# State-space pipeline beside the projections, key selection regrouped and its passes pinned in a queue

## The chip, the core and the metric

The kernel runs on one core of a Trainium2 chip. The core has five engines, each with its own queue, worked off in order: TensorE (PE: matmuls and transposes; PEld in the profile is its weight load), VectorE (DVE), ScalarE (ACT), GpSimd (POOL), and SyncE (SP), which here only starts transfers. On-chip memory is SBUF, and PSUM for TensorE's results. The metric is the time of one execution in microseconds (us), as the median of several.

## The reference

One decoder block on 2048 tokens of 1024 channels, in float32: RMSNorm with adaptive shift and scale, one wide input projection, two branches, a gated merge, an output projection, and a SwiGLU feed-forward part.

```python
u = rms_norm(h, norm1_g[layer]) * (1.0 + scale1) + shift1
xs, q, ckv, qi, ki, wi, ga, gb = split_cols(u @ w_in[layer], IN_SIZES)
y_ssm = s5_branch(xs, ...)          # state-space branch
y_att = dsa_branch(q, ckv, qi, ki, wi, ...) @ w_attn_proj[layer]
merged = jax.nn.sigmoid(ga) * y_ssm + jax.nn.sigmoid(gb) * y_att
h = h + gate1 * (merged @ w_out[layer])
u2 = rms_norm(h, norm2_g[layer]) * (1.0 + scale2) + shift2
ffn = (jax.nn.silu(u2 @ w_ffn_gate[layer]) * (u2 @ w_ffn_up[layer])) @ w_ffn_down[layer]
```

The state-space branch is a diagonal linear recurrence over time in 32 groups of 16 channels (64 states each), then GELU, then a gated linear unit (`y @ w_glu`, "GLU" below). The attention branch selects keys first: per query, four small index heads give a score for every earlier key, and the 256 highest are kept:

```python
rel = jax.nn.relu(jnp.einsum('bqhd,bkd->bqhk', qi, k_idx))
iscore = jnp.einsum('bqhk,bqh->bqk', rel, wi)
_, sel = lax.top_k(iscore, topk)            # topk = 256
```

Attention with eight heads then runs over the selected keys alone.

## The kernel before, in words

Matmuls run in a fast float32 type; each operand is split in a high and a low part, so one product is three matmuls (`mm3`, high x high, high x low, low x high), all issued at line 102. The stages, in order of time:

1. **Input projections** (`main_A`). `w_in` is taken in column blocks of 128, the tokens in four quarters of 512. One output tile `pps` of 128x512 takes 24 matmuls (8 blocks of the contraction x 3) into one of three PSUM banks, and one eviction on ScalarE: `kraw`, `qio`, `xsT`, `craw` for keys, index queries, state-space input and latent, `qo` (L648) for queries, `go` (L654, a sigmoid) for the two gates `ga`, `gb`. There are 112 tiles. Weights come as `wraw` on SP's queue, are rounded to `wh` on ScalarE (L433), and `wl` is the rest, on GpSimd (L113). The tokens' operands are `U` and `Uh`.
2. **Key selection** (`select_group`, L730 on), for blocks of 128 queries, 2 to 15 (a block b sees (b+1) x 128 keys). Scores: `sps` on TensorE, relu `rl` on ScalarE (L713), weighted sum `SC` on VectorE (L718). Then a search for the threshold: in each pass ScalarE counts, row by row, the scores above a bound (`ja`, L766, a Sign with an accumulated sum, one instruction per block), and VectorE moves the bounds (`tsel`, L768 to L782, some twelve short instructions). Then the nearest scores (`near`, L800), and the mask (`gt`). Several blocks form a group that shares the short instructions; 11 passes per group, 14 for the smallest blocks. Two lists of groups run beside each other (`GROUPS`).
3. **State-space operators** (`ssm_build`): GpSimd multiplies (`sE`, `sT`, `sW`, `sO`), ScalarE and VectorE split them (`opt`), SP stores them to `scratch_opd` and `scratch_etd`.
4. **State-space pipeline** (`main_ssm`): 16 steps of two groups each ("pairs"), staged over eleven further steps. For a pair: loads of `sxc`, `oph`, `sEt` on SP, transposes `sxp`, split `XHL` (ScalarE, VectorE), matmuls `sup` (12), rotation `sZ` (VectorE, GpSimd), a scan along time on VectorE (`ZS`), `sP` (GpSimd), split `PHL`, matmuls `syp` (18), GELU `sY` (ScalarE, L1237), transposes `sbp` and `syt`, copies `YC` and `sy`.
5. **GLU** (`main_glu`, tiles `ggp`, `gvp`), then **attention**, **merge**, **feed-forward**.

What runs beside what is fixed while the program is written out. `beside(main, ...)` takes steps of a main generator and, for each, gives every background generator credit of its step's nominal time x a rate; a background runs while it has credit. `BR` is the rate of the operators, `SR` that of the two lists of groups, and the number that a step yields is what it is charged. A scheduler then puts each engine's instructions in order by a model of its own; it may move an instruction ahead of others that were written earlier. `keep_in_program_order` forbids that for one instruction: it stays behind the one that was written before it on its engine.

Before, projections run with the operators, both lists of groups, and `lead()`, which starts the pipeline's first ten yields when 14 or fewer steps of the projections are left. Then the pipeline runs on its own, then the GLU with what is left of selection.

Buffers come from rings of equal slots: `big` (tag p8, 9 slots of 8 KB per partition), `half` (h4, 27 of 4 KB), `qtr` (q2, 12 of 2 KB).

Of the kernel before, what the change touches and what calls it, by code (L numbers as in the profile page):

```python
# [36 lines left out]
BR = 0.6  # L37
SR = (0.55, 0.55)
# [6 lines left out]
LEAD = (14, 10, 6)  # L45
# [13 lines left out]
GROUPS = ((((7, 6), 11), ((15,), 11), ((13,), 11)), (((5, 4, 3, 2), 14), ((14, 12, 10), 11), ((11, 9, 8), 11)))  # L59


class Kernel:
# [667 lines left out]
    def select_group(self, bs, passes, then):  # L730
# [33 lines left out]
        for p in range(passes):  # L764
            for i in range(nb):
                A.activation(junk[:, :W_[i]], S_[i], AF.Sign, bias=T[:, 0, i:i + 1], accum_out=C[:, i:i + 1])  # L766
            yield sum(W_) * CTA + 0.1 * nb + 0.8
# [17 lines left out]
            yield 0.5  # L785
# [8 lines left out]
        for i in range(nb):  # L794
            W = W_[i]
            n = -(-W // 512)
            for c in range(n):
                s = S_[i][:, c * 512:min((c + 1) * 512, W)]
                y = self.qtr([128, 512], "near")[:, :s.shape[1]]
                A.activation(y, s, AF.Sign, bias=far[:, i:i + 1], scale=-1.0)  # L800
                V.scalar_tensor_tensor(y, y, FAR, s, op0=OP.mult, op1=OP.min)
                V.max(m8[:, nb + c if n > 1 else i], y)
            if n > 1:
                V.max(m8[:, i], m8[:, nb:nb + n])
            yield W * CFIN[0]
# [334 lines left out]
    def main_ssm(self):  # L1140
# [4 lines left out]
        def load(bt, kinds):  # L1145
            for kind in kinds:
                op[bt, kind] = t = self.half([128, 2, 4, 128], "oph", F32R)
                S.dma_start(t.bitcast(F32), self.opd[bt, :, kind].rearrange("p w (g x) -> p w g x", x=128))
# [8 lines left out]
        def split_x(p):  # L1157
            if p % 2 == 0:
                R = op[p // 2, 1].bitcast(F32)
                RS = self.half([128, 2, 4, 128], "RS", F32R)  # L1160
                G.tensor_scalar(RS[:, :, :, :64], R[:, :, :, 64:], 1.0, 1.0, op0=OP.mult, op1=OP.mult)
                G.tensor_scalar(RS[:, :, :, 64:], R[:, :, :, :64], -1.0, 1.0, op0=OP.mult, op1=OP.mult)
                op[p // 2, 4] = RS

# [1109 lines left out]
    def run(self, stop=99):  # L2274
        tc = self.tc
        self.stores, self.now, self.qpre, self.left, self.xsT = [], 0.0, {}, 99, {}
        with ExitStack() as st:
# [38 lines left out]
            def select(groups):  # L2316

                for g, (bs, passes) in enumerate(groups):
                    while self.seg < 1 or max(bs) >= 8 and (self.ready < 2 or self.E16 is not None):
# [30 lines left out]
            def lead():  # L2350

                while self.left > LEAD[0] or build[0] is not None:
                    yield None
                for _ in range(LEAD[1]):
                    yield next(ssm) * LEAD[2]

# [55 lines left out]
```

## Time and profile before

| | us |
|---|---|
| median of three runs | 3326.09 (3324.31 to 3326.35) |
| profiled execution | 3328.0 |
| its span (first to last instruction) | 3326.2 |
| TensorE busy | 3109.1 (93%) |
| VectorE busy | 2263.7 (68%) |
| ScalarE busy | 1558.8 (47%) |
| GpSimd busy | 1548.1 (47%) |
| projections, first matmul to end of last | 49.5 to 938.1 |
| pipeline, until the GLU's first matmul | 938.1 to 1062.9 |

TensorE's busy time counts overlapping matmuls as one stretch; a matmul's own duration (some 0.39 us for 512 columns) is longer than the distance to the next one. The granted clock (PEclk) is the share of its full rate that TensorE was given. A wait is put down to the instruction that ended it. In the views, "L102 PE" with a tile's name tells the stage, since every matmul has that line.

### The profile page before, as it was taken

Reading aid. Unit: us, or ns where it says so; the run is one execution under the profiler, and the core shown is the slowest. Engines: PE = TensorE matmul, PEld = TensorE weight load, DVE = VectorE, ACT = ScalarE, POOL = GpSimd, SP = SyncE. Lnnn points to the kernel's source line nnn. Section 1 sums busy time; section 2 is a strip of 40 time slices with the busy share of each in tenths; the row PEclk is TensorE's granted clock in tenths of the full one; section 3 lists DMA queues with packets and bytes.
Section 4 is the critical chain, followed back from the end, with each engine's and each line's share of the span. In section 5 each row is a group of like instructions: output and inputs, shape, how many; then the busy total and the mean of one; then the engine's idle time right before and its main releaser. Section 6 shows DMA issues by size and latency. Waiting matters only on the chain.

```text
span 3326.2 us, 44918 instructions
## 1 busy us (share of the span) xinstructions
PE 3109.1 (93%) x15346; PEld 2572.7 (77%) x15346; DVE 2263.7 (68%) x4617; ACT 1558.8 (47%) x2758; POOL 1548.1 (47%) x1200
## 2 busy tenths in 40 slices
PE   5988778999988999999989999999999999999998
PEld 2776656777877888888978887888878888888786
DVE  6778567866366848888974548666676666755576
ACT  3335656695644327888952234323333223332233
POOL 2465534623156656666651235555564545200533
PEclk8999889999998999999999999999999999999999
DMA  7533323564366771000154665333443333665464
GB/s 242 165 102 118 108 91 137 202 203 141 104 237 242 260 236 60 20 20 20 36 169 155 193 219 173 99 101 106 139 135 115 108 95 99 228 221 162 144 224 143
DMA packets 386680, 479.97 MB, mean 144 GB/s; under 512 B 38208, under 2 KB 264720, under 8 KB 384784
## 3 DMA queue, kind: packets, MB, share of 16 engines
q1 hardware_dynamic: 373200, 452.95, 42.1%
q10 hardware_dynamic: 13248, 24.12, 2.0%
q8 instruction: 121, 1.98, 0.2%
q14 instruction: 111, 0.91, 0.1%
HBM read 311.77 MB, written 165.22 MB: 143 GB/s over the span
## 4 chain that ended last, share of the span: by engine, by line
PE 65%; DVE 9%; DMA 5%; issue 4%; ACT 4%; POOL 3%; SPq 0%; ACTq 0%; DVEq 0%; POOLq 0%
PE fps L102 25%; PE dps L102 7%; PE wops L102 5%; PE pps L102 5%; PE aps L102 4%; PE pvo L102 4%; PE ptp L110 3%; PE apj L102 3%; PE ggp L102 3%; PE gvp L102 3%; DMA bw<-in_w_ffn_down_dram 2%; ACT ja L766 2%; DVE SC L718 1%; PE kps L102 1%; PE sps L102 1%
## 5 line engine op out<-in xcount | busy, mean ns | idle before, releaser
L102 PE MATMUL fps<-X,wp 128*128 128x512 f32 x3696 | 865.6, 396 | 11.1 <-POOL wp L113 4.1
L102 PEld LDWEIGHTS fps<-X,wp 128*128 128x128 f32 x3696 | 697.8, 189 | 175.7 <-POOL wp L113 5.0
L102 PE MATMUL pps<-Uh,wh 128*128 128x512 f32 x1120 | 361.8, 401 | 22.1 <-ACT qo L648 15.4
L102 PE MATMUL dps<-db,dh 128*128 128x512 f32 x1056 | 324.8, 390 | 6.2 <-ACT db L2053 5.0
L113 POOL TENSOR_TENSOR wl<-wraw,wh 128x1024 fp32r<-128x1024 f32 x72 | 180.2, 2505 | 301.4 <-ACT wh L433 251.6
L102 PEld LDWEIGHTS pps<-Uh,wh 128*128 128x128 f32 x1120 | 214.2, 193 | 69.1 <-ACT qo L648 15.9
L102 PE MATMUL pps<-U,wh 128*128 128x512 f32 x672 | 228.2, 419 | 39.4 <-ACT go L654 22.0
L766 ACT ACTIVATE ja<-SC,tsel 128x1152 int8<-128x1152 f32 (+11 forms) x166 | 210.2, 1268 | 85.4 <-DVE tsel L782 73.5
L102 PEld LDWEIGHTS dps<-db,dh 128*128 128x128 f32 x1056 | 197.7, 188 | 49.9 <-ACT db L2053 7.3
L113 POOL TENSOR_TENSOR wp<-wraw,wp 128x512 fp32r<-128x512 f32 x88 | 131.7, 1506 | 198.9 <-ACT wp L1911 198.9
L102 PE MATMUL pps<-Uh,wl 128*128 128x512 f32 x560 | 223.7, 400 | 0.0
L1518 POOL TENSOR_SCALAR P<-P,sum 128x1024 f32<-128x1024 f32 (+2 forms) x192 | 170.5, 900 | 83.8 <-DVE sum L1515 72.1
L102 PE MATMUL dps<-db,dl 128*128 128x512 f32 x528 | 204.3, 389 | 0.0
L113 DVE TENSOR_TENSOR pl<-ptp,ph 128x512 fp32r<-128x512 f32 (+1 forms) x288 | 183.9, 655 | 27.5 <-ACT ph L1572 25.2
L102 PEld LDWEIGHTS pps<-U,wh 128*128 128x128 f32 x672 | 133.1, 201 | 74.0 <-ACT go L654 22.8
L102 PE MATMUL wops<-wo,M 128*128 128x512 f32 x768 | 184.9, 397 | 0.0
L1959 POOL TENSOR_TENSOR c<-c,c 128x512 f32<-128x512 f32 x66 | 88.7, 1344 | 195.2 <-issue 133.5
L110 PE MATMUL ptp<-shift,P 128*128 128x128 f32 x1088 | 169.6, 278 | 10.2 <-POOL P L1518 6.7
L1572 ACT CAST ph<-ptp 128x512 fp32r<-128x512 f32 (+1 forms) x288 | 156.1, 563 | 49.0 <-PE ptp L110 45.0
L102 PE MATMUL aps<-K,Qh 128*128 128x512 f32 (+3 forms) x640 | 173.5, 378 | 2.6 <-DVE mx L1505 2.6
L102 PEld LDWEIGHTS wops<-wo,M 128*128 128x128 f32 x768 | 142.4, 188 | 32.0
L102 PE MATMUL pvo<-pl,Vt 128*128 128x256 f32 x576 | 165.5, 317 | 0.0
(455 smaller groups left out, 7128.1 us busy)
## 6 DMA issues: line engine op xcount, KB each, us to landing
draw<-scratch_hp SPq DMA_DIRECT2D x66, 512.0 KB, 4.6
bw<-in_w_ffn_down_dram SPq DMA_DIRECT2D x121, 256.0 KB, 3.9
wraw<-in_w_in_dram SPq DMA_DIRECT2D x56, 512.0 KB, 5.3
scratch_hp<-c SPq DMA_DIRECT2D x110, 256.0 KB, 2.0
wraw<-in_w_ffn_gate_dram SPq DMA_DIRECT2D x44, 512.0 KB, 6.4
wraw<-in_w_ffn_up_dram SPq DMA_DIRECT2D x44, 512.0 KB, 6.9
scratch_opd<-opt SPq DMA_DIRECT2D x32, 512.0 KB, 3.0
oph<-scratch_opd SPq DMA_DIRECT2D x32, 512.0 KB, 6.4
```

Source lines behind the costliest of these rows:

```text
L102: self.T.matmul(ps, lhsT, rhs, start=start, stop=stop)
L110: self.T.transpose(out, in_, self.ident)
L113: (eng or self.V).tensor_tensor(out, src, hi.bitcast(F32), op=OP.subtract)
L718: V.scalar_tensor_tensor(sc, r, self.WI[:, b, h:h + 1], sc if h else more, op0=OP.mult, op1=OP.add)
L766: A.activation(junk[:, :W_[i]], S_[i], AF.Sign, bias=T[:, 0, i:i + 1], accum_out=C[:, i:i + 1])
L1518: G.tensor_scalar(c, c, sm[:, 1:2], 1.0, op0=OP.mult, op1=OP.mult)
L1572: A.copy(ph[:, :o], ps[:, :o])
L1959: G.tensor_tensor(z, c, z, op=OP.mult)
```

## The change

- **Pipeline.** `lead()` no longer waits for the end of the projections: it waits until the operators are built and both lists of groups are done, and then offers all of the pipeline's steps beside the projections, each charged at 0.9 of its time. What is not done by the end of the projections runs after them, as before.
- **Its buffers.** The operator of kind 1 and its rotated copy `RS` now share one 8 KB slot (`oph1`), in place of two 4 KB ones.
- **Groups.** The first list is (7, 6), (15, 14), (11, 10), the second (5, 4, 3, 2), 13, 12, 9, 8: eight groups in place of six. Blocks from 8 on no longer wait for the end of the operators' first phase, which frees an 8 KB slot.
- **Rates.** `SR` from 0.55 to 0.9, with a pass charged more (0.2 per block + 1.0 in place of 0.1 + 0.8, and 1.5 in place of 0.5 for the short instructions); `BR` from 0.6 to 0.8.
- **Pin.** `ja` and `near` stay behind what was written before them on ScalarE.

Line numbers of the changed kernel are one to seven higher (L766 becomes L768, L654 L655, L1237 L1244).

```diff
-BR = 0.6
-SR = (0.55, 0.55)
+BR = 0.8
+SR = (0.9, 0.9)
...
-LEAD = (14, 10, 6)
+LEAD = 0.9
...
-GROUPS = ((((7, 6), 11), ((15,), 11), ((13,), 11)), (((5, 4, 3, 2), 14), ((14, 12, 10), 11), ((11, 9, 8), 11)))
+GROUPS = ((((7, 6), 11), ((15, 14), 11), ((11, 10), 11)),
+          (((5, 4, 3, 2), 14), ((13,), 11), ((12,), 11), ((9,), 11), ((8,), 11)))
...
-                A.activation(junk[:, :W_[i]], S_[i], AF.Sign, bias=T[:, 0, i:i + 1], accum_out=C[:, i:i + 1])
-            yield sum(W_) * CTA + 0.1 * nb + 0.8
+
+                self.tc.keep_in_program_order(A.activation(
+                    junk[:, :W_[i]], S_[i], AF.Sign, bias=T[:, 0, i:i + 1], accum_out=C[:, i:i + 1]))
+            yield sum(W_) * CTA + 0.2 * nb + 1.0
...
-            yield 0.5
+            yield 1.5
...
-                A.activation(y, s, AF.Sign, bias=far[:, i:i + 1], scale=-1.0)
+                self.tc.keep_in_program_order(A.activation(y, s, AF.Sign, bias=far[:, i:i + 1], scale=-1.0))
...
             for kind in kinds:
-                op[bt, kind] = t = self.half([128, 2, 4, 128], "oph", F32R)
+                if kind == 1:
+                    both = self.big([128, 2, 2, 4, 128], "oph1")
+                    t, op[bt, 4] = both[:, 0], both[:, 1]
+                else:
+                    t = self.half([128, 2, 4, 128], "oph", F32R)
+                op[bt, kind] = t
...
-                RS = self.half([128, 2, 4, 128], "RS", F32R)
+                RS = op[p // 2, 4]
...
-                    while self.seg < 1 or max(bs) >= 8 and (self.ready < 2 or self.E16 is not None):
+                    while self.seg < 1 or max(bs) >= 8 and self.ready < 2:
...
-                while self.left > LEAD[0] or build[0] is not None:
+                while build[0] is not None or any(g[0] is not None for g in sel):
                     yield None
-                for _ in range(LEAD[1]):
-                    yield next(ssm) * LEAD[2]
+                for t in ssm:
+                    yield t * LEAD
```

How this moves instructions is seen in the written order of each engine. ScalarE in the projections, before; the rows are the passes of blocks 5 to 2 (128x768 to 128x384) after a gate's eviction `go`, with the store of `go`:

```order
L654 ACTIVATE go<-pps 128x512
L766 ACTIVATE ja,tsel<-SC,tsel 128x640
L655 DMA scratch_sga<-go 128x512
L766 ACTIVATE ja,tsel<-SC,tsel 128x512
L766 ACTIVATE ja,tsel<-SC,tsel 128x384
L766 ACTIVATE ja,tsel<-SC,tsel 128x768
L766 ACTIVATE ja,tsel<-SC,tsel 128x640
L766 ACTIVATE ja,tsel<-SC,tsel 128x512
L766 ACTIVATE ja,tsel<-SC,tsel 128x384
```

Three more rounds of four and two `near` follow before the next `go`: 19 passes. In the changed kernel the passes of these blocks and of 7 and 6 (128x1024, 128x896) stand around the queries' evictions `qo`:

```order
L649 ACTIVATE qo<-pps 128x512
L768 ACTIVATE ja,tsel<-SC,tsel 128x896
L768 ACTIVATE ja,tsel<-SC,tsel 128x384
L650 DMA scratch_qT<-qo 128x512
L768 ACTIVATE ja,tsel<-SC,tsel 128x1024
L768 ACTIVATE ja,tsel<-SC,tsel 128x768
L768 ACTIVATE ja,tsel<-SC,tsel 128x896
L768 ACTIVATE ja,tsel<-SC,tsel 128x640
L768 ACTIVATE ja,tsel<-SC,tsel 128x512
L768 ACTIVATE ja,tsel<-SC,tsel 128x384
```

The next `qo` stands 24 passes and two `near` after this one. Further on, where blocks 15 and 14 (128x2048, 128x1920) and block 13 (128x1792) are searched at once, ScalarE's queue in the changed kernel ends a run of ten passes like this:

```order
L768 ACTIVATE ja,tsel<-SC,tsel 128x1792
L768 ACTIVATE ja,tsel<-SC,tsel 128x2048
L768 ACTIVATE ja,tsel<-SC,tsel 128x1920
L768 ACTIVATE ja,tsel<-SC,tsel 128x2048
L768 ACTIVATE ja,tsel<-SC,tsel 128x1920
L768 ACTIVATE ja,tsel<-SC,tsel 128x1792
L803 ACTIVATE near<-SC,tsel 128x512 x3
L803 ACTIVATE near<-SC,tsel 128x256
L655 ACTIVATE go<-pps 128x512 x2
```

Two evictions then stand together. Before, block 15 was a group of its own, block 13 came after it in the same list, and 14 went with 12 and 10 in the other.

ScalarE in the state-space pipeline, before: no eviction of the projections is left, and one table load (the engine's function table is exchanged when GELU follows another set's function) serves all GELUs:

```order
L655 DMA scratch_sgb<-go 128x512
L1185 CAST XHL<-sxp 128x512 x2
L1219 CAST PHL<-sP 128x1024
L1185 CAST XHL<-sxp 128x512
L1237 ACT_TABLE_LOAD
L1237 ACTIVATE sY<-syp 128x512
L1185 CAST XHL<-sxp 128x512
L1219 CAST PHL<-sP 128x1024 x2
L1185 CAST XHL<-sxp 128x512
L1237 ACTIVATE sY<-syp 128x512
```

In the changed kernel sigmoid evictions and GELUs alternate, each behind a table load:

```order
L655 ACT_TABLE_LOAD
L655 ACTIVATE go<-pps 128x512
L1244 ACT_TABLE_LOAD
L1244 ACTIVATE sY<-syp 128x512
L1226 CAST PHL<-sP 128x1024
L656 DMA scratch_sgb<-go 128x512
L1257 COPY YC<-sbp 128x16x32
L1192 CAST XHL<-sxp 128x512
L655 ACT_TABLE_LOAD
L655 ACTIVATE go<-pps 128x512
L1244 ACT_TABLE_LOAD
L1244 ACTIVATE sY<-syp 128x512
```

The whole program has 24 table loads, where it had 8. TensorE at the same place, before (the pipeline begins behind the last projection matmul):

```order
L102 MATMUL pps<-Uh,wh 128x512 x2
L102 MATMUL pps<-Uh,wl 128x512
L110 MATMUL sxp<-shift,sxc 128x128 x8
L102 MATMUL sup<-XHL,oph 128x256
L102 MATMUL sup<-XHL,RS 128x256
L102 MATMUL sup<-XHL,oph 128x256 x5
```

and in the changed kernel, some tiles ahead of the end of the projections:

```order
L103 MATMUL pps<-Uh,wl 128x512
L103 MATMUL sup<-XHL,oph_7998 128x256 x10
L103 MATMUL pps<-Uh,wh 128x512 x2
L103 MATMUL pps<-Uh,wl 128x512
L103 MATMUL pps<-Uh,wh 128x512 x2
L103 MATMUL pps<-Uh,wl 128x512
L111 MATMUL sbp<-shift,sY 128x8x16 x4
L111 MATMUL sxp<-shift,sxc 128x128 x4
L103 MATMUL pps<-U,wh 128x512 x2
```

The pipeline's matmuls now stand between projection matmuls, from tile 92 or 93 on. The scores `sps`, which before reached to tile 98, end before tile 88.

More of the change, by code (lines that the diff above doesn't have):

```diff
@@ L1159, in split_x @@
                 R = op[p // 2, 1].bitcast(F32)
-                RS = self.half([128, 2, 4, 128], "RS", F32R)
+                RS = op[p // 2, 4]
                 G.tensor_scalar(RS[:, :, :, :64], R[:, :, :, 64:], 1.0, 1.0, op0=OP.mult, op1=OP.mult)
                 G.tensor_scalar(RS[:, :, :, 64:], R[:, :, :, :64], -1.0, 1.0, op0=OP.mult, op1=OP.mult)
-                op[p // 2, 4] = RS
         def load_e(p):
```

## The prediction

> **What bounds the kernel now.** I read the page's busy shares first, then the windows of the first 1260 us cut at the marks of the program, then TensorE's waits, and last the timeline where the longest wait lies. "Tile" below means one 128x512 output of the input projections (`pps`): 24 matmuls and one eviction on ScalarE, 112 in all.
>
> ```profile
> PE 3109.1 (93%) x15346; PEld 2572.7 (77%) x15346; DVE 2263.7 (68%) x4617; ACT 1558.8 (47%) x2758; POOL 1548.1 (47%) x1200
> 217.80:415.00 197.20, 163.56 (x713) 130.72 (x711) 143.43 (x401) 118.56 (x264) 101.35 (x74) 0.93 0.35 111
> 415.00:692.00 277.00, 231.56 (x1048) 188.85 (x1049) 207.63 (x515) 178.83 (x297) 133.70 (x90) 0.91 0.45 153
> 692.00:819.40 127.40, 122.42 (x526) 98.79 (x525) 81.01 (x284) 94.67 (x145) 37.25 (x15) 0.97 0.51 157
> 819.40:938.10 118.70, 118.70 (x527) 97.30 (x526) 38.33 (x150) 78.35 (x122) 12.13 (x9) 1.00 0.35 119
> 938.10:1062.90 124.80, 97.18 (x673) 88.02 (x671) 90.53 (x110) 54.08 (x78) 83.56 (x77) 0.90 0.67 241
> 1062.90:1260.00 197.10, 196.20 (x872) 159.05 (x872) 120.93 (x130) 65.53 (x99) 119.04 (x71) 0.98 0.78 257
> ```
>
> Columns: window, its length, busy us of PE, PEld, DVE, ACT, POOL, granted clock, DMA share, GB/s. TensorE is the bound overall. The change can win only where TensorE pauses or runs at a lowered clock: 217.8 to 819.4 (tiles 20 to 91, the "middle") and 938.1 to 1062.9 (the state-space pipeline alone). At 819.4 to 938.1 it is never idle, and from 1062.9 on hardly. In the middle it is idle for 84.1 us (601.6 minus 517.5), and the clock withheld (0.07 x 197, 0.09 x 277, 0.03 x 127) is another 43 us. Half of that idle time has one cause:
>
> ```profile
> PE pps L102 <- ACT go L654: 22.8, 3, 20.4
> PE pps L102 <- ACT qo L648: 19.7, 4, 15.4
> PE sps L102 <- ACT rl L713: 14.6, 6, 6.3
> ```
>
> (Total, times, longest.) TensorE waits for ScalarE to empty a bank. The 20.4 us looks like this on the two engines:
>
> ```profile
> 421.95 0.57 ACT L654 ACTIVATE go<-pps 128x512 f32<-128x512 f32 x1
> 426.45 0.94 ACT L766 ACTIVATE ja<-SC,tsel 128x768 int8<-128x768 f32 x1 [1.52 <-DVE tsel L782]
> 431.54 0.93 ACT L766 ACTIVATE ja<-SC,tsel 128x768 int8<-128x768 f32 x1 [1.52 <-DVE tsel L782]
> 448.53 0.57 ACT L654 ACTIVATE go<-pps 128x512 f32<-128x512 f32 x1
> 428.37 0.39 PE L102 MATMUL pps<-Uh,wl 128*128 128x512 f32 x1
> 449.15 1.22 PE L102 MATMUL pps<-U,wh 128*128 128x512 f32 x2 [20.40 <-ACT go L654]
> 428.00:449.00 21.00, 0.76 (x4) 0.29 (x2) 6.64 (x43) 13.87 (x33) 1.10 (x1) 0.60 0.00 0
> ```
>
> Between two `go` evictions ScalarE's queue holds rounds of key selection for blocks 5, 4, 3, 2. A round takes 5.09 us (426.45 to 431.54), of which 1.52 is the wait for VectorE's next threshold. The 26.6 us from 421.95 to 448.53 cost TensorE 20.4, so only 5.8 to 6.2 us, about one tile, was in hand. The clock falls to 0.60 as well.
>
> **The state-space pipeline, main gain.** Before, it runs alone and is paced by its own chain:
>
> ```profile
> POOL sZ L1202 <- DVE sZ L1201: 26.4, 5, 20.0
> ACT sY L1237 <- PE syp L102: 21.7, 10, 6.4
> L1237 ACT ACTIVATE sY<-syp x16: 587/598/642, 956.8 to 1054.5; 128x512 f32<-128x512 f32 x16
> 996.21 0.52 PE L102 MATMUL syp<-XHL,oph 128*128 128x256 f32 x3
> 996.56 1.61 PE L102 MATMUL syp<-PHL,oph 128*128 128x256 f32 x12
> 998.01 0.52 PE L102 MATMUL syp<-XHL,oph 128*128 128x256 f32 x3
> 999.31 0.60 PE L110 MATMUL sbp<-shift,sY 128*128 128x128 f32 x4
> 999.75 0.60 PE L110 MATMUL syt<-shift,YC 128*128 128x128 f32 x4
> 427.01 0.39 PE L102 MATMUL pps<-Uh,wl 128*128 128x512 f32 x1
> 427.24 0.62 PE L102 MATMUL pps<-Uh,wh 128*128 128x512 f32 x2
> 427.69 0.39 PE L102 MATMUL pps<-Uh,wl 128*128 128x512 f32 x1
> 1062.90 0.51 PE L102 MATMUL ggp<-Y,wh 128*128 128x512 f32 x1 [2.05 <-ACT Y L1309]
> ```
>
> Sixteen GELUs (`sY`, one per pair of groups) from 956.8 to 1054.5 are one per 6.5 us, and 8.4 us follow until the GLU's first matmul. Start to start, a 256-column matmul takes 0.121 us (996.56 to 998.01 over twelve), a transpose 0.11 (four in 0.44), a projection matmul 0.227 (three in 0.68). So the pipeline's 480 matmuls and 192 transposes are 79 us of TensorE in 124.8 us of time.
>
> In the changed order, counted row by row, 306 of these matmuls and 96 transposes stand among the last 20 tiles, and eight of the GELUs come after the last projection eviction. From tile 92 on:
> - 480 projection matmuls x 0.227 = 109, 306 x 0.121 = 37, 96 x 0.11 = 11: 157 us back to back;
> - the rest alone at the old pace, seven gaps x 6.5 + 8.4 = 54 us;
> - friction in the mix: no row shows it. From below nothing (tiles 92 to 111 had no idle time with 46 score matmuls among them), from above 20 us (the 84.1 idle over 72 tiles, times 20 tiles, is 23). I take 4, nearer the row of the same tiles, since selection is over by then and VectorE and GpSimd are light (38.33 and 12.13 us in 118.7).
>
> That is 215 against 243.5 us (819.4 to 1062.9). But the 46 score matmuls that stood behind tile 92 now stand ahead of it:
>
> ```profile
> 818.94 0.62 PE L102 MATMUL sps<-K,Qg 128*128 128x512 f32 x2
> 819.40 0.63 PE L102 MATMUL pps<-U,wh 128*128 128x512 f32 x2
> ```
>
> 0.23 each, 10 us more in the middle. Net gain 28 - 10 = **18 us**.
>
> What moves with it: 16 further table loads, because GELUs and sigmoid evictions now alternate.
>
> ```profile
> L1237 ACT ACT_TABLE_LOAD x1 | 1.3, 1283 | 0.0
> L433 ACT CAST wh<-wraw 128x1024 fp32r<-128x1024 f32 x72 | 75.1, 1048 | 35.4 <-DMA wraw<-in_w_ssm_glu_dram 18.4 <-DMA wraw<-in_w_in_dram 6.6 <-DVE macc L272 3.5
> ```
>
> 16 x 1.28 = 20.5 us of ScalarE. Per 5.5 us tile ScalarE has 0.6 (eviction) + 0.5 (half a `wh`) + about 2.3 (three of five of a pair's casts, GELU and copies, some 3.5 us) + 1.3 (loads): 4.7 against TensorE's 157/20 = 7.9. So I cost them at nothing. Without that cover they would cost up to 20.5. The Trainium skill, "ScalarE: Activation LUTs", section "Table sets: the hidden batching unit", says to do all calls of one set before switching, which this change undoes, and counts about 2.7 us a load. By that figure, an estimate, ScalarE would carry 43 us rather than 20.5 there; the row's 1283 ns decides.
>
> On SP's queue the pipeline's loads now stand between the weight loads (`wraw`). Together they are 0.35 x 118.7 + 0.67 x 124.8 = 125 us of full DMA use over 211 us, 0.59, below the 0.67 that the pipeline had alone: nothing, if weights still come one tile pair ahead. `RS` and the shift copies change only their buffer: nothing.
>
> **Selection and operators, the middle.** Rounds of selection rise from 69 (five groups x 11 + 14) to 91, so VectorE gets 22 more chains of 1.5 us, 33 us. And all passes now end before tile 92, behind which 49 us of ScalarE's passes stood (first row below: L766 alone, from tile 92 to the last tile). ScalarE's order shows what the pin and the new grouping do to runs between evictions:
>
> ```profile
> 819.40:938.10 118.70, 49.16 (x66) 1.00 0.35 119
> L766 ACT ACTIVATE ja<-SC,tsel 128x2048 int8<-128x2048 f32 x11 | 22.0, 2003 | 23.5 <-DVE tsel L782 20.1 <-DVE tsel L784 3.2 <-DVE tsel L759 0.2
> L766 ACT ACTIVATE ja<-SC,tsel 128x1920 int8<-128x1920 f32 x11 | 20.9, 1897 | 10.6 <-DVE tsel L782 9.4 <-DVE tsel L784 1.1
> L766 ACT ACTIVATE ja<-SC,tsel 128x1792 int8<-128x1792 f32 x11 | 19.6, 1786 | 1.2 <-DVE tsel L782 1.2
> L766 ACT ACTIVATE ja<-SC,tsel 128x768 int8<-128x768 f32 x14 | 13.0, 931 | 20.3 <-DVE tsel L782 16.5 <-DVE tsel L780 3.4 <-DVE tsel L778 0.4
> ```
>
> Before, two long runs (15 and 19 passes) cost 15.4 and 20.4 us. Now there is one run of 24 passes of the small blocks: 21.6 us of passes (means of 0.61 to 1.14 us) and three uncovered waits of 1.52, about 26 us, hence again about 20 of stall. And there is one of ten passes of blocks 15, 14 and 13, which take turns and so hide each other's wait: 4 x 1.79 + 3 x 2.00 + 3 x 1.90 + 2 of `near` = 21 us, less 5.8 in hand, 15. Together 35 against 36: I take the middle as even, 0 us. Its bounds: if the pin ends the waits for `go` and `qo`, 42.5 us and their half of the withheld clock, 64 us less. If the denser load adds, then by the rows ScalarE's work exceeds TensorE's at two places: in tiles 32 to 35 by 15 us (33 passes of the small blocks with casts and evictions, 38, against four tiles of 5.5 and a few transposes, 23), in tiles 52 to 55 by 22 (16 passes of blocks 13 to 15, eight `near`, casts and evictions, 45 or 46, against 24). That is 37, and with the same half of clock 55 us more.
>
> The faster operators (0.6 to 0.8) move GpSimd's 1.1 to 1.3 us multiplies forward: the last one now stands before weight tile 28 instead of 38. They delay `wl`, whose waits on TensorE are the smallest named; nothing taken, inside the upper bound.
>
> **Sum.** 3326.2 (span) - 18 + 0 = 3308. The profiled execution took 3328.0, 1.8 above its span, and the median of the three is 3326.1, 1.9 below that execution, so the span equals the median and I predict **3308 us**.
>
> **The rivals.**
> 1. The pin pays. For: passes were hoisted ahead of evictions, as at 421.95. Against: the run of 24 is still there. From half to all of the 64, taken at 45: 3326 - 18 - 45 = 3263, between 3244 and 3276.
> 2. Slower: ScalarE becomes the middle's bound. Place: tiles 32 to 56, where both groups pass at once and the operators' casts come too. Each pass taken earlier stands ahead of an eviction; it decides once ScalarE has more than TensorE between evictions, which it has in the two places above. For: 55 more microseconds by the upper bound. Against: tiles 56 to 91 then have less left, and 35 us of their loss could go. 3326 - 18 + 37 = 3345, up to 3363.
> 3. The overlap gives nothing: a GELU waits for its matmuls (21.7 us in all before) and blocks the next sigmoid eviction behind a table load, and TensorE's own queue holds projections behind a pipeline matmul that isn't ready. With friction at its upper 20, 231 instead of 215: 3326 - 12 + 10 = 3324; with nothing hidden, 243.5 and the 10 more before: 3336. In between: 3328, no change or a little slower. Against: the pipeline's longest waits (20 us on `sZ`) are GpSimd's and VectorE's, which the projections hardly use there.
>
> **How the numbers follow.** Forecast 0.45, rival 1 0.23, rival 2 0.20, rival 3 0.12. A measurement tells 0.2%, 6.6 us, from no change. Faster by more: 0.37 of the forecast's 0.45, all of rival 1: 0.60. Within: 0.05 of the forecast, 0.07 of rival 3, 0.01 of rival 2: 0.13. Slower: 0.03, 0.05 and 0.19: 0.27. The forecast's own range is 3290 to 3332 (friction 0 to 20, the middle 14 better to 8 worse); for 8 in 10 I go on to the values of rivals 1 and 2: 3262 to 3346.
>
> **What would show it.** Right: the last projection matmul 161 us after tile 92's first (118.7 before), the GLU's first matmul near 1045 instead of 1062.9, eight GELUs before the last eviction, tiles 92 to 111 with TensorE above 95% busy, and the idle time of the middle near 84 us with two ScalarE stalls of 15 to 20 us. Wrong: more than 110 us idle in the middle (rival 2), under 50 (rival 1), or a span from tile 92 to the GLU above 230 us (rival 3). The time from the GLU to the end must stay as it is, 2263 us; if it moves by more than 7 us I have missed something.

## The result: 1.2% slower, and the profile after

The changed kernel takes 3365.9 us (median of four, 3363.5 to 3373.5) against 3325.2 us for the kernel before beside it: 1.0124 of its time, 95% interval 1.0111 to 1.0137. The profiled execution of the changed kernel took 3363.5 us with a span of 3361.7, so the trace accounts for 35.5 of the 41 us.

Busy times of the page, and windows of the first 1260 us, cut as before (window, length, busy us of PE, PEld, DVE, ACT, POOL, granted clock, DMA share, GB/s). Tile 20 begins at 230.4, tile 56 at 634.2, tile 92 at 903.9; the last projection ends at 1061.8 and the GLU begins at 1105.4.

```profile
PE 3114.8 (93%) x15346; PEld 2570.8 (76%) x15346; DVE 2279.2 (68%) x4891; ACT 1579.7 (47%) x2774; POOL 1533.4 (46%) x1200
```

```profile
47.90:230.40 182.50, 147.70 (x641) 116.33 (x642) 147.88 (x395) 56.52 (x118) 106.48 (x85) 0.89 0.46 146
230.40:634.20 403.80, 308.32 (x1321) 244.15 (x1319) 304.76 (x891) 263.63 (x495) 195.95 (x141) 0.85 0.35 120
634.20:903.90 269.70, 239.25 (x1008) 191.00 (x1009) 190.25 (x775) 192.93 (x312) 49.73 (x24) 0.95 0.44 139
230.40:903.90 673.50, 547.58 (x2329) 435.15 (x2328) 495.01 (x1665) 456.57 (x806) 245.68 (x165) 0.89 0.39 128
903.90:1061.80 157.90, 157.90 (x885) 136.63 (x884) 59.00 (x78) 70.98 (x87) 76.01 (x65) 1.00 0.60 199
1061.80:1105.40 43.60, 36.00 (x270) 33.06 (x268) 27.14 (x35) 26.02 (x37) 21.72 (x21) 0.89 0.72 252
1105.40:1260.00 154.60, 154.25 (x682) 125.12 (x683) 83.61 (x74) 47.44 (x74) 93.16 (x53) 0.99 0.76 249
```

The same cuts in the trace of before, where they were not shown yet:

```profile
49.50:217.80 168.30, 142.61 (x641) 114.13 (x642) 133.81 (x404) 56.41 (x118) 91.58 (x71) 0.91 0.48 151
217.80:819.40 601.60, 517.54 (x2285) 418.36 (x2284) 432.06 (x1200) 392.06 (x704) 272.30 (x178) 0.93 0.43 140
819.40:1062.90 243.50, 215.88 (x1197) 185.31 (x1195) 128.86 (x260) 132.43 (x200) 95.68 (x86) 0.95 0.52 182
```

Read downwards, in us:

| stretch | before | after | difference |
|---|---|---|---|
| start to tile 20 | 217.8 | 230.4 | +12.6 |
| the middle, tiles 20 to 91 | 601.6 | 673.5 | +71.9 |
| tile 92 to the GLU | 243.5 | 201.5 | -42.0 |
| GLU to the end | 2263.3 | 2256.3 | -7.0 |

The overlap came, and paid 42. The middle took back 72. In it TensorE is idle for 125.9 us (673.5 minus 547.6) where it was 84.1, and its busy time is 30 longer. Of that, 10 are the score matmuls that moved ahead of tile 92 (260 of the 304 started in the middle before, all do now: 44, not the 46 of the prediction), and about 20 are matmuls that run longer at a lower clock (0.89 granted, 0.93 before).

TensorE's waits in the middle (total, times, longest):

```profile
PE pps L103 <- ACT go L655: 34.0, 5, 18.5
PE pps L103 <- ACT qo L649: 31.6, 4, 23.7
PE sps L103 <- ACT rl L714: 21.7, 18, 3.6
PE pps L103 <- ACT xsT L590: 9.8, 2, 9.0
```

The same names as before, each larger; the fourth was this one:

```profile
PE pps L102 <- ACT xsT L589: 2.4, 1, 2.4
```

Summed over all rows of the two views, ScalarE ended 71 us of TensorE's waits before and 107 after, VectorE 13 and 18. The longest looks like this (ScalarE's and TensorE's timelines, then windows over it):

```profile
377.15 0.57 ACT L649 ACTIVATE qo<-pps 128x512 f32<-128x512 f32 x1
...
387.76 0.93 ACT L768 ACTIVATE ja<-SC,tsel 128x768 int8<-128x768 f32 x1 [1.52 <-DVE tsel L785]
...
392.85 0.93 ACT L768 ACTIVATE ja<-SC,tsel 128x768 int8<-128x768 f32 x1 [1.52 <-DVE tsel L785]
...
407.48 0.57 ACT L649 ACTIVATE qo<-pps 128x512 f32<-128x512 f32 x1
```

```profile
408.11 1.22 PE L103 MATMUL pps<-U,wh 128*128 128x512 f32 x2 [23.70 <-ACT qo L649]
```

```profile
384.50:408.10 23.60, 0.00 (x0) 0.00 (x0) 10.38 (x65) 18.37 (x42) 2.15 (x2) 0.60 0.00 0
408.10:412.00 3.90, 3.89 (x9) 3.12 (x10) 3.87 (x11) 2.32 (x5) 2.92 (x4) 0.50 0.44 137
```

Thirty microseconds lie between two evictions, filled with the passes of the small blocks, and TensorE does nothing for 23.6 of them. ScalarE itself is busy for 18.4 of these. Afterwards the clock is at 0.50 for some 4 us more, so a stall costs more than its own length. The Trainium skill, "TensorE: Matmul & The Clock Gate", section "What's actually happening", says that the clock falls to half after an idle window of about 3.4 us; the granted 0.50 behind this stall agrees.

The pipeline's part shows two further things: the eighth of the sixteen GELUs (`sY`) runs before the last eviction (`go`), and the table loads alternate.

```profile
1045.10 0.60 ACT L1244 ACTIVATE sY<-syp 128x512 f32<-128x512 f32 x1
...
1061.83 0.60 ACT L655 ACTIVATE go<-pps 128x512 f32<-128x512 f32 x1 [3.03 <-PE pps L103]
```

```profile
L655 ACT ACT_TABLE_LOAD x9 | 11.5, 1283 | 0.2
L1244 ACT ACT_TABLE_LOAD x9 | 11.5, 1283 | 0.2
```

### The profile page after: what moved, and what is told of

It reads as the page before. It is cut to its first block, busy times and chain, and to the rows that moved or that the text cites. A ratio compares the mean times of both kernels' runs of the same rounds, so it can differ in the third digit from the quotient of the medians.

```text
span 3361.7 us, 45242 instructions
## 1 busy us (share of the span) xinstructions
PE 3114.8 (93%) x15346; PEld 2570.8 (76%) x15346; DVE 2279.2 (68%) x4891; ACT 1579.7 (47%) x2774; POOL 1533.4 (46%) x1200
## 4 chain that ended last, share of the span: by engine, by line
PE 67%; DVE 14%; ACT 7%; issue 4%; DMA 3%; POOL 3%; SPq 0%; DVEq 0%; ACTq 0%; POOLq 0%
PE fps L103 24%; PE dps L103 7%; PE pps L103 7%; PE wops L103 5%; PE aps L103 4%; ACT ja L768 4%; PE pvo L103 4%; PE ptp L111 3%; PE apj L103 3%; PE ggp L103 3%; PE gvp L103 3%; DVE SC L719 2%; DMA bw<-in_w_ffn_down_dram 2%; PE kps L103 1%; PE syp L103 1%
## 5 line engine op out<-in xcount | busy, mean ns | idle before, releaser
L103 PE MATMUL pps<-Uh,wh 128*128 128x512 f32 x1120 | 358.7, 399 | 25.6 <-ACT go L655 11.2
L103 PE MATMUL pps<-U,wh 128*128 128x512 f32 x672 | 239.9, 440 | 66.3 <-ACT qo L649 30.7
L768 ACT ACTIVATE ja<-SC,tsel 128x1024 int8<-128x1024 f32 (+13 forms) x166 | 210.2, 1267 | 90.4 <-DVE tsel L785 59.0
L114 POOL TENSOR_TENSOR wp<-wraw,wp 128x512 fp32r<-128x512 f32 x88 | 131.1, 1500 | 199.5 <-ACT wp L1918 199.5
L103 PEld LDWEIGHTS pps<-U,wh 128*128 128x128 f32 x672 | 140.8, 214 | 103.1 <-ACT qo L649 32.0
L1579 ACT CAST ph<-ptp 128x512 fp32r<-128x512 f32 (+1 forms) x288 | 156.0, 563 | 44.9 <-PE ptp L111 40.4
```

The source lines that it names most:

```text
L103: self.T.matmul(ps, lhsT, rhs, start=start, stop=stop)
L114: (eng or self.V).tensor_tensor(out, src, hi.bitcast(F32), op=OP.subtract)
L768: self.tc.keep_in_program_order(A.activation(junk[:, :W_[i]], S_[i], AF.Sign, bias=T[:, 0, i:i + 1], accum_out=C[:, i:i + 1]))
L1579: A.copy(ph[:, :o], ps[:, :o])
```

## The experiments

In all tables "middle" is the first matmul of tile 20 to that of tile 92, and "92 to GLU" runs on from there to the GLU's first matmul, both from the profiled execution. Ratios are to the kernel before, on the same chip.

### One part of the change undone at a time

Four kernels, each the changed one with one part put back:

```diff
 u_pin     -  self.tc.keep_in_program_order(A.activation(...))    +  A.activation(...)
 u_br      -  BR = 0.8                                            +  BR = 0.6
 u_groups  -  GROUPS (eight groups), gate without E16             +  GROUPS (six groups), gate with E16
 u_lead    -  pipeline begins when operators and selection end    +  LEAD = (14, 10, 6), as before
```

> The changed kernel without the pin on ja and near (3366 with it). Theory A (too much selection and operator work before tile 92, whatever its order): the middle (tiles 20 to 91, 673 us) keeps to within 15 us, 3350 to 3380. Theory B (the pin holds passes ahead of evictions and makes the two long runs): the stalls of 24 and 18 us go, 42 us and their clock, about 3310.

> The changed kernel with the operators' rate back at 0.6; the pipeline still starts beside the projections. Theory A, operators' share: tiles 8 to 19 get back 12 us and tiles 28 to 56 some 20 to 30, while tiles 56 to 72 lose 10: 3335 to 3350. If the rate of the operators doesn't matter (selection alone makes the loss): 3360 to 3370.

> The changed kernel with the six groups of before (and the gate on the operators' first phase). Theory A: 22 rounds of VectorE's short instructions fewer, 33 us of VectorE, and the middle 10 to 20 us shorter; the pipeline starts two tiles later, 4 us: 3350 to 3360. If the run of ten passes of blocks 13 to 15 is what the grouping costs, its 18 us and the clock go too: 3335 to 3345.

> The changed kernel with the pipeline started only at the end of the projections, as before. Both theories: the middle stays at 673 us to within 5, and the stretch from tile 92 to the GLU goes back from 201 to 235 to 244 us: 3400 to 3410. If the overlap had caused part of the middle's loss through buffers, the middle would shrink.

| kernel | median | ratio, 95% | to tile 20 | middle | 92 to GLU |
|---|---|---|---|---|---|
| changed | 3365.9 | 1.0124 (1.0111 to 1.0137) | 230.4 | 673.5 | 201.5 |
| u_pin | 3365.5 | 1.0122 (1.0106 to 1.0139) | 229.6 | 672.7 | 199.5 |
| u_br | 3377.1 | 1.0158 (1.0141 to 1.0175) | 215.5 | 697.9 | 199.5 |
| u_groups | 3380.2 | 1.0164 (1.0147 to 1.0181) | 230.6 | 673.4 | 212.6 |
| u_lead | 3399.0 | 1.0220 (1.0203 to 1.0237) | 230.4 | 678.5 | 230.2 |

The pin does nothing: without it the middle is as long, to 0.8 us. The overlap is worth 33 us (u_lead against the changed kernel). The new groups are worth 14: with the six old ones the middle is the same, though it has 22 rounds fewer, but the pipeline gets less done before the last projection. The faster operators cost 15 us before tile 20, and pay 24 in the middle; that slower ones meet the dense selection later is my reading, not tested apart. I had expected the old groups to be faster and the slower operators to be faster or equal, and both came out slower. None of these four is where the 72 us went.

### The rate of the selection alone

```diff
 u_sr      -SR = (0.9, 0.9)    +SR = (0.55, 0.55)     and the old charges: 0.1 * nb + 0.8, 0.5
 a_sr07    -SR = (0.9, 0.9)    +SR = (0.7, 0.7)       new charges
 b_sr      -SR = (0.55, 0.55)  +SR = (0.9, 0.9)       the kernel BEFORE with this rate and the new charges alone
```

> The changed kernel with selection's rate and charges as before (0.55; 0.1 per block + 0.8 and 0.5); operators at 0.8, new groups and pin stay. Selection then reaches to tile 100 and the pipeline doesn't start beside the projections. Theory A2 (the rate of selection makes the middle's loss): the middle falls from 673 to 600 to 630 us while tile 92 to GLU goes back to about 240: 3325 to 3350. If the rate isn't the cause (groups of eight and operators are): middle stays 650 or more, 3370 to 3400.

> The changed kernel with selection's rate at 0.7 and the new charges: selection reaches to tile 102, the pipeline's transposes begin at tile 103. Theory A2: the middle 610 to 640 us, tile 92 to GLU about 235: 3325 to 3350. If the loss doesn't hang on the rate: middle 660 or more, 3385 or more.

> The kernel before with selection's rate at 0.9 and the new charges, nothing else: selection ends at tile 81 instead of 98. Theory A2: the middle rises from 602 by 50 to 80 us and nothing is won behind it but 10 us of scores: 3365 to 3400. If the rate alone is harmless: 3315 to 3335.

| kernel | median | ratio, 95% | middle | 92 to GLU |
|---|---|---|---|---|
| u_sr | 3331.1 | 1.0016 (1.0006 to 1.0025) | 596.8 | 241.1 |
| a_sr07 | 3345.0 | 1.0053 (1.0036 to 1.0070) | 618.6 | 232.7 |
| b_sr | 3399.9 | 1.0215 (1.0195 to 1.0236) | 682.4 | 235.1 |

The rate, with its charges, is the cause of the loss in the middle, and it is shown both ways. With the old rate put back the changed kernel's middle falls by 77 us, and the overlap goes, since selection then reaches past tile 100. The kernel before with the new rate alone loses 81 us in the middle. Windows of the kernel with the old rate, and of the kernel before with the new one:

```profile
229.30:826.10 596.80, 518.82 (x2306) 421.89 (x2305) 445.09 (x1364) 405.70 (x728) 247.75 (x161) 0.93 0.42 138
```

```profile
217.50:899.90 682.40, 546.00 (x2329) 438.08 (x2328) 467.02 (x1315) 439.39 (x777) 260.37 (x175) 0.88 0.37 125
```

What TensorE waits for there is not the same in every kernel. The largest row of the kernel with the old rate, then the two largest of the kernel before with the new one:

```profile
PE Tps L103 <- DVE tsel L775: 19.8, 1, 19.8
```

```profile
PE Tps L102 <- DVE nst L1095: 30.8, 4, 21.4
PE pps L102 <- ACT go L654: 26.0, 3, 18.4
```

Over all rows, with the old rate ScalarE ends only 18 us of waits and VectorE 58. In the kernel before with the new rate they end 78 and 54, so there 41 of the 52 us of idle time that came on top stand behind VectorE (13 before). ScalarE's queue is the main place of the stalls in the changed kernel, but the rate loads VectorE's queue too.

### What in the selection costs the time

All these are the changed kernel with the rate kept, and one load of the search taken out. None makes the exact repair of rows, and the thresholds that they find mean nothing. In the changed kernel the repair's place is at 1246 us, behind the middle. m_nowait has ten small buffers instead of twelve, to make room for its second count.

```diff
 m_nowait   bias=T[:, 0, i:i + 1], accum_out=C[:, i:i + 1]  ->  bias=self.NV[:, i:i + 1], accum_out=CC2[:, p % 2, i:i + 1]
 m_nochain  the updates of the thresholds on VectorE left out; bias=self.NV[:, i:i + 1]
 m_short    junk[:, :W_[i]], S_[i]  ->  junk[:, :128], S_[i][:, :128]
```

> The changed kernel in which a pass of the key selection no longer waits for the threshold of the round before: its bias is a constant and its count goes to one of two buffers in turn, so VectorE's update of a round may follow a round later. All passes on ScalarE and all updates on VectorE stay, in the same places of the order. Left out: the search itself (the thresholds that it finds mean nothing) and the exact repair of rows. In the changed kernel the middle (tiles 20 to 91) takes 673 us with TensorE idle for 126, and ScalarE's passes wait 84 us there for a threshold. Theory R, the round trip at the head of ScalarE's queue is what stalls TensorE: waits of passes for a threshold nearly gone, the middle at 585 to 615, the run near 3295. Theory L, the passes' own time on ScalarE ahead of the evictions: the middle at 655 to 675. Theory V, VectorE's queue is too full: also 655 to 675.

> The changed kernel with the updates of the search left out on VectorE (some 10 small instructions a round, 91 rounds) and a constant bias in the passes: ScalarE's passes stay, neither waits nor updates remain. The exact repair of rows is left out too. Theory R: the middle as without the waits alone, 585 to 615, and nothing more. Theory V: 40 us or more below the kernel without the waits alone, since VectorE's 496 us of work in the middle fall by some 90 to 130. Theory L: 655 to 675, since ScalarE has as many passes as before.

> The changed kernel in which every pass counts over the first 128 keys alone, so that ScalarE's passes fall from 0.6 to 2.0 us to about 0.3 each; the waits for a threshold and VectorE's updates stay, in the same places. Left out: the counts over the other keys and the exact repair of rows. Theory L: the middle at 590 to 615, the run near 3300. Theory R: part of it, since a round still takes its 1.5 us turn on VectorE but the pass is shorter: 625 to 650. Theory V: 655 to 675.

| kernel | ScalarE's passes | VectorE's updates | passes wait for the threshold | median | middle |
|---|---|---|---|---|---|
| changed | full | yes | yes | 3365.9 | 673.5 |
| m_nowait | full | yes | hardly (10.9 us) | 3310.5 | 625.0 |
| m_nochain | full | none | hardly (7.0 us) | 3279.2 | 585.8 |
| m_short | 128 keys | yes | yes | 3308.2 | 611.8 |

Windows of the middle of these three, in this order:

```profile
231.80:856.80 625.00, 537.35 (x2330) 431.63 (x2328) 502.41 (x1667) 455.53 (x806) 242.67 (x165) 0.93 0.42 137
```

```profile
229.80:815.60 585.80, 531.77 (x2330) 428.90 (x2329) 372.74 (x706) 451.35 (x806) 247.13 (x165) 0.93 0.44 147
```

```profile
229.80:841.60 611.80, 530.61 (x2329) 427.78 (x2328) 503.37 (x1666) 317.35 (x806) 242.26 (x165) 0.93 0.43 140
```

No single theory holds. The round trip alone is worth 48 us (the expectation R said 585 to 615 in the middle, and it is 625). With VectorE's updates left out as well it is 39 more (V asked for 40), with ScalarE as full as ever. ScalarE's passes by themselves are worth 62 (L). The first and the last, each taken out alone, give 110 together, more than the 72 us lost, so they are not parts that add up; and each also takes out what the search cost before the change. How the 72 divide among passes, waits and updates stays open.

The time of the passes is not the whole price either. With short passes ScalarE spends 143 us less in them (79.34 in the row below, 222.14 in the changed kernel), and the middle falls by 62: 0.43 us for each.

```profile
229.80:841.60 611.80, 79.34 (x332) 0.93 0.43 140
```

ScalarE's waits for the threshold in the changed kernel, then in the one with short passes:

```profile
ACT ja L768 <- DVE tsel L785: 59.0, 35, 5.2
...
ACT ja L768 <- DVE tsel L787: 19.3, 4, 7.8
```

```profile
ACT ja L768 <- DVE tsel L785: 81.4, 34, 8.5
...
ACT ja L768 <- DVE tsel L787: 20.8, 6, 9.3
```

With short passes ScalarE waits longer for thresholds (102 against 78 us in these rows), and yet the middle is 62 us shorter. I read this so: a wait at the head of ScalarE's queue hurts where passes and waits together exceed what is in hand between two evictions, and a wait with little work behind it doesn't. No run tests that apart.

A kernel with 6 and 7 instead of 11 and 14 passes a group (78 of 166 passes, 103 us of ScalarE by the trace, and the exact repair left out) was meant to tell the same, and did not:

> The changed kernel with about half of the counting passes (6 for 11, 7 for 14) and the exact repair behind them switched off, so that selection finds its thresholds less closely: leaves out some 76 passes of 166 on ScalarE, about 96 us, and 39 of 91 round trips. Its pipeline starts at tile 71. Theory A (ScalarE's and VectorE's load of selection makes the middle's stalls): the projections and the pipeline together, tile 20 to GLU, 875 us, get shorter by 80 to 120 us. If the stalls come from elsewhere (operators, GpSimd, weights): by under 40.

It took 3347.1 us (1.0061, 1.0040 to 1.0083). Tile 20 to the GLU took 857.7 us against 875.0, only 17 less: in its order each group followed sooner on the one before, the last score matmul stands in tile 65 and the last pass in tile 69 (85 and 90 in the changed kernel). The passes per tile, which were to be halved, fell by a fifth, from 2.6 (166 passes in tiles 26 to 90) to 2.1 (88 in tiles 26 to 69), and the whole pipeline moved in among the projections. So it settles nothing.

### Can the density be put where it does no harm?

The operators' multiplies, casts and transposes share VectorE and ScalarE with the selection up to about tile 56. So the rate was raised only once they were built:

```diff
-SR = (0.9, 0.9)                     +SR = (0.55, 0.55), old charges
+    while build[0] is not None:
+        yield None
+    for b in sel:
+        b[1] = 0.8
     while any(g[0] is not None for g in sel):
```

> The changed kernel with the selection at the old rate and charges (0.55) as long as the operators are being built, and at 0.8 from then on. In the order the last score matmul stands behind weight tile 87 and the pipeline's first transposes behind tile 95, as in the changed kernel (85 and 95), so the overlap is kept. Theory of the collision (dense selection stalls TensorE only where the operators' multiplies, casts and transposes share VectorE and ScalarE with it): tiles 20 to 55 as with the old rate, 358 us (404 in the changed kernel); tiles 56 to 91 at 245 to 270; from tile 92 to the GLU 200 to 210; the run at 3295 to 3315, below both kernels. Theory of density alone (as many passes per tile stall as much wherever they stand): tiles 56 to 91 take 300 us or more, the run at 3345 to 3365.

3381.9 us, 1.0163 (1.0148 to 1.0177). Tiles 20 to 55, then 56 to 91:

```profile
229.70:587.40 357.70, 291.63 (x1322) 237.13 (x1321) 290.65 (x703) 218.21 (x446) 201.95 (x142) 0.89 0.40 136
587.40:901.30 313.90, 243.33 (x1010) 194.10 (x1008) 198.60 (x913) 231.89 (x351) 46.76 (x23) 0.89 0.36 119
```

The first part is that of the old rate, to the digit (206.0 + 151.7 = 357.7 in u_sr). The second took 313.9 instead of 239.0 (108.3 + 130.7), 75 us more, with GpSimd busy for only 46.76 of it. The passes alone, in the two parts of this kernel and then in the second part of the one with the old rate (u_sr):

```profile
229.70:587.40 357.70, 88.30 (x172) 0.89 0.40 136
587.40:901.30 313.90, 129.02 (x154) 0.89 0.36 119
```

```profile
587.00:826.10 239.10, 99.04 (x115) 0.97 0.45 144
```

Here 30 us of passes more went with 75 us of time. In the changed kernel's tiles 20 to 55, beside the operators, 45 us more (133.3 against 88.2) went with 46. My hope to have both was wrong: a dense selection without the operators beside it is no cheaper, and here it was dearer. The run as a whole came out slower than even the theory of density had it.

### Less density than before

If the price is density, the old rate may already be too high. c1 keeps of the change only the new groups, the pin and the buffer of `RS`; c2 and c3 lower the rate too; b_rate050 is the kernel before with the lower rate alone.

```diff
 c1_rate055   SR = (0.55, 0.55), old charges, BR = 0.6, LEAD = (14, 10, 6) in the changed kernel
 c2_rate050   the same, SR = (0.5, 0.5)
 c3_rate045   the same, SR = (0.45, 0.45)
 b_rate050    -SR = (0.55, 0.55)  +SR = (0.5, 0.5)  in the kernel before
```

> The changed kernel with the selection at the old rate and charges (0.55), the operators at the old rate (0.6) and the old beginning of the pipeline: of the change the new groups, the pin and the buffer of RS are left. By the runs so far the middle costs what the selection's density asks (597 us at 0.55, 619 at 0.7, 674 at 0.9) and the operators' 13 us before tile 20 come back. Theory that density alone decides, whatever the grouping: the middle at 595 to 605, tile 92 at 812 to 822, from tile 92 to the GLU 235 to 245, the run at 3318 to 3330. Theory that the new groups are a cost of their own at the old rate (22 more rounds): the middle at 620 or more, the run at 3340 or more.

> As c1_rate055, with the selection's rate at 0.50, so that its last score matmul stands behind weight tile 107 instead of 100. If the middle's loss grows with density at every level, also below 0.55: the middle 8 to 15 us shorter than at 0.55, of which the last 20 tiles take back less than half since TensorE was never idle there: the run 5 to 10 us below c1_rate055, at 3312 to 3322, below the kernel before. If 0.55 is already where the loss ends: equal to c1_rate055 within 3 us.

> As c2_rate050 with the selection's rate at 0.45: 24 of the 304 score matmuls now stand behind the last projection, beside the GLU. If the loss grows with density at every level and the rest hides behind the GLU: the middle at 560 to 577, the run 5 to 20 us below c2_rate050, at 3280 to 3294. If selection that is not done by the last projection is late for the attention or stalls the GLU: 3300 or more.

> The kernel before with the selection's rate at 0.50 instead of 0.55 and nothing else; its last score matmul stands behind weight tile 106 instead of 98. If the loss grows with density also below 0.55: 5 to 12 us below the kernel before. If not: within 3 us of it.

| kernel | median | ratio, 95% | middle | 92 to GLU | GLU to end |
|---|---|---|---|---|---|
| c1_rate055 | 3320.0 | 0.9978 (0.9969 to 0.9987) | 606.6 | 234.2 | 2257.6 |
| c2_rate050 | 3298.7 | 0.9913 (0.9899 to 0.9927) | 577.1 | 235.4 | 2261.7 |
| c3_rate045 | 3311.7 | 0.9954 (0.9941 to 0.9968) | 562.0 | 241.5 | 2285.8 |
| b_rate050 | 3328.4 | 1.0006 (0.9997 to 1.0015) | 586.4 | 259.7 | 2262.7 |

c2 beats both kernels: 0.9% below the one before, 2.0% below the changed one. It gained more on c1 than expected (21 us instead of 5 to 10); c3 missed its 3280 to 3294 and met the other theory, that selection left for later is late; b_rate050 stayed within 3 us of the kernel before, though its middle fell. The rows of the passes alone (L766 or L768, length of the window, ScalarE's time in them, twice their number), middle first, then to the GLU, for c2 and c3:

```profile
216.40:793.50 577.10, 167.55 (x257) 0.94 0.44 147
793.50:1028.80 235.30, 49.65 (x68) 0.96 0.54 191
```

```profile
217.10:779.10 562.00, 157.03 (x244) 0.95 0.45 147
779.10:1020.60 241.50, 50.62 (x66) 0.96 0.53 188
```

and the middle of the kernel before, of the changed one, and of the changed one with the old rate (u_sr):

```profile
217.80:819.40 601.60, 173.13 (x266) 0.93 0.43 140
```

```profile
230.40:903.90 673.50, 222.14 (x332) 0.89 0.39 128
```

```profile
229.30:826.10 596.80, 187.25 (x285) 0.93 0.42 138
```

and of c1:

```profile
217.70:824.30 606.60, 192.43 (x291) 0.91 0.42 138
```

From c2 to the changed kernel 54.6 us of passes more in the middle go with 96 us of time, 1.8 us for each; from the kernel before it is 49.0 for 72 (1.5), from u_sr 34.9 for 77 (2.2). That is the price of the rate, with all that it moves (waits, updates, scores), counted by its passes; it is not the price of a pass, which the short passes put at 0.43. Nor does it hold between all kernels: against the one before, u_sr has 14 us of passes more and a middle 5 us shorter, c1 has 19 more and is 5 longer. In the last 20 tiles and the pipeline passes are nearly free: c2 has 49.65 us of them there and c1 29.67, for 235.4 against 234.2 us. At 0.45 the middle falls by another 15 us, but 24 score matmuls and their passes are then left for the GLU and the attention, and the end takes 24 us longer. In the kernel before, with its old groups, the lower rate moves as much out of the middle (15 us) and loses it from tile 92 to the GLU (16): there the larger groups stand in the pipeline's way. So the lower rate pays only with the new groups (new groups alone, c1: 7 us; the lower rate alone: nothing; both: 29); that the groups' size is the reason is argued, not tested apart.

## Why the prediction was wrong

1. **"I take the middle as even, 0 us"** is the step that failed. It weighed two long runs of passes before (15.4 and 20.4 us of stall) against two after (20 and 15 predicted). Both were found rightly: 23.7 us on `qo` at 384, in tiles 32 to 35, and 18.5 us on `go` at 616, in tiles 52 to 55. But they are 42 of 126 us of idle time, and the sum left the rest as it was: outside the two runs the idle time was 48 us before and is 84 now. Idle time grew by 42 in all, and the clock with it (withheld, as 1 minus the granted clock times its length: 42.7 us before, 73.4 after). What did it is the raised rate: alone in the kernel before it costs 81 us in the middle (b_sr), and taken back in the changed kernel it gives 77 (u_sr). The passes in the middle rose from 173 to 222 us of ScalarE, which stood in the rows that the prediction itself quoted (49.16 us behind tile 92, all to be pulled forward), and I let that weigh nothing outside the two runs. It measured +72 us with the 10 of the score matmuls in it, which my sum had apart: +62 where I said 0, beyond my upper bound of 55. The bounds of 64 and 55 took half of the idle time for the clock as well, which is too much: of the 42.7 us withheld before, only 25.6 fell in time in which TensorE worked.

2. **The overlap** was right in kind and too small in size: 215 us predicted from tile 92 to the GLU, 201.5 measured. The friction that I set at 4 us, no row showing it, is none: 157.90 us busy of 157.90, at a clock of 1.00, against my 157 back to back (161 with friction). The rest alone took 43.6 us where "seven gaps x 6.5 + 8.4" gave 54. The eight remaining GELUs came closer together than at the old pace (from 1063.7 to 1097.0, one per 4.8 us instead of 6.5); that their matmuls were further ahead is my reading. Net worth: 33 us by u_lead, in which the score matmuls stand in the middle as well, where I had 18.

3. **The table loads** cost nothing, as predicted: 16 more (9 + 9 instead of 1 + 1 in these two lines) at 1283 ns each, and the 16 that stand among the last 20 tiles lie in a stretch where TensorE was never idle. In that stretch a load begins at most 19 ns behind the end of the instruction before it, and a GELU starts 11 ns after it, so a switch takes some 1.31 us. The 2.7 us a load that the Trainium skill, "ScalarE: Activation LUTs", section "Table sets: the hidden batching unit", counts is seen in no row here.

4. **The operators, "nothing taken"**, was wrong in its place: 12.6 us more up to tile 20, a stretch that I left out of the sum entirely. Idle time there rises from 25.7 to 34.8 us (windows of tiles 0 to 19, length minus PE). u_br gives these back and loses more later, so in the changed kernel the faster operators are a net gain of 11 us.

5. **The rivals.** Rival 2 named the sign, two of the places and nearly the size (3345, up to 3363; the median is 3365.9, the profiled span 3361.7), at a chance of 0.20. Its mechanism, ScalarE having more work than TensorE between evictions, holds in those two places (ScalarE busy 34.1 us and TensorE 23.8 in tiles 32 to 35, 40.4 and 25.6 in tiles 52 to 55); e_ramp shows that the loss needs neither those places nor the operators. Its "against", that tiles 56 to 91 give back 35 of the loss, failed: they took 269.7 us where the kernel before took 273.5 (146.3 + 127.3), so they gave 4. Rival 1 (the pin pays) is refuted by u_pin, rival 3 (no overlap) by the window that is busy throughout. The mark I set for rival 2, over 110 us idle in the middle, was met with 126.

6. **GLU to the end** was to stay within 7 us of 2263 and came 7.0 lower. The kernel without the overlap (u_lead) has 2262.4, which would put it down to the overlap. But c1, which begins its pipeline as before, has 2257.6, and u_groups, which overlaps, 2262.3. The cause stays open.

## What to carry to other kernels

When a planner's rate is raised so that side work ends earlier, price the whole of what moves into the dense stage, not only the longest runs that the order shows: here the raised rate cost 1.5 to 2.2 us for each microsecond of passes that it brought into the middle, though ScalarE was busy for only two thirds of that stage, and the passes' own time was the smaller part of it. An engine's busy share says little when it evicts for the bound engine; the question to ask is how much work and waiting can stand between two evictions, against what is in hand. And what is won by an overlap has to be compared with the cost of making room for it: here 42 against 72, and the better kernel was found by keeping the new groups and turning the same number the other way.

## What was not expected of the hardware

The withheld clock goes with the idle time of the middle: 29.0 of 54.7 us (c3), 35.8 of 61.5 (c2), 42.7 of 84.1 (before), 73.4 of 125.9 (changed). Over all kernels here it is 0.47 to 0.66 of the idle time, and 0.76 in m_nochain. Much of it falls into the stalls themselves, as in the 23.6 us above at 0.60, where it costs nothing more. Summed over TensorE's busy time alone, it is 25.6 us before and 43.9 in the changed kernel, 0.30 and 0.35 of the idle time. From one to the other, 42 us more of idle time came with 18 us more of it. A stall that can be removed is thus worth some 1.3 to 1.4 times its length here, an estimate from these figures.

TensorE took projections, transposes and 256-column matmuls mixed for 158 us, busy throughout at a granted clock of 1.00, with sixteen table loads on ScalarE beside it.
